# Attention keys in one ring tile, score pieces of up to 512 columns, and 64 weight columns for the lower part of some value blocks

## The chip, the cores and the metric

The kernel runs on one core of one Trainium2 chip. The metric is the device time of one execution in microseconds. A time is the median of several runs of the same kernel; the profile is one further execution, taken by the hardware profiler, with a time of its own.

## What is computed

One layer of a streaming encoder for 1024 prompt rows and 64 sample rows, all in float32, with 1024 channels. The change touches the two attentions of the prompt alone: eight heads of band attention (A) and eight heads of forgetting attention (B), each with 64 channels to a head.

```python
def attend(q, k, v, bias, mask):
    logits = jnp.einsum('bqhd,bkhd->bhqk', q, k).astype(jnp.float32) * scale
    ...
    p = jax.nn.softmax(logits, axis=-1)
    return jnp.einsum('bhqk,bkhd->bqhd', p.astype(v.dtype), v)
...
# A: each 64-frame chunk attends to itself and the 8 chunks before it, with a learned relative bias
# B: causal, swept in 128-query blocks, bias = cum[query] - cum[key] of the forget logits
oa = chunk_band_attn_prompt(qa, ka, va, rel_bias[l])
ob = forget_attn_prompt(qb, kb, vb, logf)
xp = xp + jnp.concatenate([oa, ob], axis=-1) @ w_o[l]
```

Before it stands the projection h @ w_in that makes q, k and v; behind it an output projection, a cross-attention into 256 memory tokens, and a feed-forward part with a short convolution.

## The kernel before

**Precision.** A float32 number is split into a higher part and a lower part ("hi" and "lo"), both of the type fp32r, which TensorE takes in one pass. A product of two split numbers is made of three matmuls (hi·hi, hi·lo, lo·hi); lo·lo is left out. In the attention the two halves of the array hold two such terms at once. A head has 64 channels, so the queries of one head stand as weights with hi in one half of the 128 partitions and lo in the other, against keys that have hi in both halves (z = 0) or lo in both (z = 1). For the values the two parts are two halves of the weight columns: v holds 64 columns of hi and 64 of lo, and the output has two halves of 64 partitions, which ACT and VectorE add at the end (L743, L744).

**Stages.** From about 30 to 545 us the eight head pairs (p = 0 to 3 are A, 4 to 7 are B) are projected, and the attention of one pair runs beside the projection of the next. From 545 us come the sample rows and the memory's keys and values, then the output projection, the cross-attention and the feed-forward part.

**One pair's attention.** The 1024 rows are eight blocks of 128. A `Group` is two blocks: its key tile `k` (L332) holds for both heads hi and lo of 256 keys, and five such tiles rotate. A group's keys are written by `group_turn` (L473 to L489): four transposes, ACT's copies (L482), VectorE's lower parts (L484), and two transfers by the SP queue (L485) that copy each head's keys to the other half of the partitions; then the queries (L487, L489). `Attn(p, g, h)` is one head's attention for the two query blocks of group g. `score(j)` (L659) makes the scores of one query block t against the key blocks w0 to t (for A at most five, for B all from the first): for each key group two matmuls (z = 0 and 1) with the same weights, of 256 columns, or of 128 where only one of the group's blocks is in the window (L677 to L682). They go into the PSUM tile `S` of two banks, of which there is one. VectorE adds the bias and takes the maximum (L685), ACT the exponential (L687), GpSimd scales (L689). `turn` (L719 to L721) transposes the weights of four key blocks at a time, and ACT and VectorE split them into pth and ptl. `sum` (L723) multiplies by the values: for each key block one matmul with pth and one with ptl, of 256 columns where both query blocks see the key block (the blocks of `self.full`), of 128 where one alone does.

**Order.** The code records the instructions; at the end `arrange` (L2050) plays them through with a table of costs and puts each engine's instructions up to the feed-forward part in the order in which that play issued them, with the program's order as priority. Its cost of a matmul (L2086) counts the columns that move, not the columns of the weights. SP issues all transfers in one queue.

Of the kernel before, what the change touches and what calls it, by code (L numbers as in the profile page):

```python
# [8 lines left out]
F32R = mybir.dt.float32r  # L9
# [6 lines left out]
P = 128  # L16
# [25 lines left out]
def hybrid_step(ctx: ExitStack, tc: tile.TileContext, i: dict, o: dict):  # L42
    nc = tc.nc
    act, dve, pool, pe = nc.scalar, nc.vector, nc.gpsimd, nc.tensor
# [56 lines left out]
    wa = heads.enter_context(tc.tile_pool(name="wa", bufs=1, side="right"))  # L101
# [225 lines left out]
    ramp.append(len(nc.cur_bb.bb.instructions))  # L327


    class Group:  # L330
        def __init__(self):
            self.k = wa.tile([P, 2, 2, 256], F32R, name="k", bufs=5)  # L332
            self.v = wa.tile([P, 2, 2, 2, 64], F32R, name="v", bufs=5)
            self.q = self.qk = None

    groups = {}
# [304 lines left out]

    mixes = {}

    class Attn:


# [12 lines left out]
        def score(self, j, sp=None):  # L659
            p, g, h = self.p, self.g, self.h  # L660
            w0, t = self.window(j)
            n = (t - w0 + 1) * P
            s = wk.tile([P, N], F32, name="s", bufs=4)
            self.s[j] = s
            if p >= 4:
                head = 2 * (p - 4) + h
                pool.tensor_scalar(s[:, :n], bias[p, h][:, :n], ctok[:, t, head:head + 1], 1.0, op0=ALU.add, op1=ALU.mult)
                pool.affine_select(out=s[:, n - P:n], in_=s[:, n - P:n], compare_op=ALU.is_ge, fill=NEG, base=0,
                                   pattern=[[-1, P]], channel_multiplier=1)
                b = s[:, :n]  # L670
            else:
                b = bias[p, h][:, 640 - n:640]
            if sp is None:
                sp = ps.tile([P, 2, 512], F32, name="S", bufs=1).rearrange("p a b -> p (a b)")
            off = (w0 % 2) * P
            q = groups[p, g].q[:, h, j * P:(j + 1) * P]
            for kg in range(w0 // 2, t // 2 + 1):  # L677
                k0, k1 = max(w0, 2 * kg), min(t, 2 * kg + 1) + 1
                a = off + (k0 - w0) * P
                src = slice((k0 - 2 * kg) * P, (k1 - 2 * kg) * P)  # L680
                for m in range(2):
                    pe.matmul(sp[:, a:a + (k1 - k0) * P], q, groups[p, kg].k[:, h, m, src], start=m == 0, stop=m == 1)  # L682
            mx = wk.tile([P, 1], F32, name="mx", bufs=4)
            sm = wk.tile([P, 1], F32, name="ssum", bufs=4)
            dve.tensor_tensor_reduce(out=s[:, :n], in0=sp[:, off:off + n], in1=b, scale=-1.0, scalar=BIG,  # L685
                                     op0=ALU.add, op1=ALU.min, accum_out=mx)
            act.activation(s[:, :n], s[:, :n], ACT.Exp, bias=mx, scale=-1.0, accum_out=sm)  # L687
            dve.reciprocal(sm, sm)  # L688
            pool.tensor_scalar(s[:, :n], s[:, :n], sm, 1.0, op0=ALU.mult, op1=ALU.mult)  # L689
# [33 lines left out]
        def sum(self, ch):  # L723
# [3 lines left out]
            if first:  # L727
                self.op = bank("O")[:, :256].rearrange("p (a b) -> p a b", a=2)
            op = self.op
            for b in sorted(ch, key=lambda b: (b != self.full[0], b)):  # L730
                cols = slice(0 if b <= a1 else 1, 2 if b >= b0 else 1)
                hi, lo, x = self.pts[b]
                for m, pt in enumerate((hi, lo)):
                    pe.matmul(op[:, cols], groups[p, b // 2].v[:, b % 2, h].rearrange("p a d -> p (a d)"),  # L734
                              pt[:, x, cols], start=b == self.full[0] and m == 0, stop=b == self.last and m == 1)
            if ch[-1] != self.last:
                return
            if h == 0:
# [767 lines left out]
    for n, u in enumerate(mems):  # L1506
        h, c = u.h, u.c
# [834 lines left out]
```

## Time and profile before

| | |
|---|---|
| median of 3 runs | 1707.46 us (1704.11 to 1709.73) |
| the profiled execution | 1703.21 us, span 1701.4 us |
| TensorE clock granted over the span | 0.998 |
| key transfers (L485) | 60, 128 KB each, 2.3 us from issue to landing |
| VectorE waiting for scores (L685 for L682) | 22.3 us in 44 waits |

The profile has for each engine a busy time, and for TensorE two rows: PE for matmuls and PEld for the loads of weights, which run beside the matmul ahead of them. Each matmul has its own weight load. Records of matmuls overlap, because they are pipelined: how long one holds the engine is read from the distance of starts, not from its duration. The views of the trace that are used below are windows (busy time of each engine in a stretch), groups by line, waits (who waited for whom), and the timeline. In a group's row "x160 | 28.2, 258 | 2.1" is the count, the busy time in us, the mean duration in ns, and the idle time ahead of it. In a timeline row the first two numbers are start and length in us, and a form `128*64` gives the rows and the columns of the weights.

### The profile page before, as it was taken

The page shows a single profiled execution, that of the slowest core. Times are in us where ns is not written, and L with a number is a line of the kernel's source. Part 1 is how long each engine was busy: PE and PEld are TensorE (multiplying, and loading weights), DVE is VectorE, ACT ScalarE, POOL GpSimd, SP SyncE. Part 2 cuts the span into 40 slices and gives each one's busy share as a digit, 9 for nine tenths or more (in the row PEclk, how much of TensorE's full clock was granted, in tenths as well). Part 3 has the DMA queues.
Part 4 walks back from the last instruction along what each step waited for, and adds up shares of the span by engine and source line. Part 5 has one row for each costly group of instructions (what it writes and reads, how often), then busy time and mean ns, then how long its engine had stood idle before and what let it go on. Part 6 is the DMA issues. An engine that isn't in the chain of part 4 may idle for free.

```text
span 1701.4 us, 33544 instructions
## 1 busy us (share of the span) xinstructions
PE 1676.9 (99%) x12264; PEld 1636.4 (96%) x12264; DVE 1158.1 (68%) x2552; ACT 906.8 (53%) x1995; POOL 583.3 (34%) x846
## 2 busy tenths in 40 slices
PE   8999999999999999999999999999999999999999
PEld 8899999999998889999999999999999999999998
DVE  7877766767777645334444697777777777659986
ACT  8757766767777565335555554333333333434442
POOL 1746647888877104434445211000000000000000
PEclk9999999999999999999999999999999999999999
DMA  8322223223146955411114642222222222983332
GB/s 258 101 57 81 75 81 103 76 77 99 48 147 189 267 186 185 139 57 51 55 58 141 211 134 83 80 78 79 77 77 77 77 79 82 306 305 122 104 108 88
DMA packets 138422, 199.84 MB, mean 117 GB/s; under 512 B 22200, under 2 KB 77624, under 8 KB 138256
## 3 DMA queue, kind: packets, MB, share of 16 engines
q1 hardware_dynamic: 138256, 197.70, 37.8%
q8 instruction: 96, 1.57, 0.4%
q14 instruction: 70, 0.57, 0.1%
HBM read 148.01 MB, written 43.34 MB: 112 GB/s over the span
## 4 chain that ended last, share of the span: by engine, by line
PE 83%; DVE 6%; ACT 5%; DMA 2%; issue 2%; POOL 1%; SPq 0%; DVEq 0%; ACTq 0%; POOLq 0%
PE W L1703 26%; PE pj L1156 14%; PE W L2027 11%; PE pj L407 11%; PE S L682 4%; PE O L734 3%; PE PT L719 3%; PE pj L802 2%; PE W L1156 2%; PE pj L529 1%; PE S L1445 1%; PE tq L1481 1%; PE O L1481 1%; PE O L1056 1%; ACT q L487 1%
## 5 line engine op out<-in xcount | busy, mean ns | idle before, releaser
L407 PE MATMUL pj<-whi,xhi 128*128 128x384 f32 (+1 forms) x480 | 175.4, 365 | 0.0
L407 PE MATMUL pj<-wlo,xhi 128*128 128x384 f32 (+1 forms) x480 | 164.7, 343 | 0.0
L407 PE MATMUL pj<-whi,xlo 128*128 128x384 f32 (+1 forms) x480 | 164.1, 342 | 0.0
L1703 PE MATMUL W<-h,hi 128*128 128x272 f32 x704 | 134.3, 288 | 1.4 <-ACT qlo L1839 1.4
L1809 POOL COPY s<-gp 128x2 f32<-128x2 f32 x22 | 15.8, 719 | 336.1 <-DVE gp L1808 336.1
L2027 PE MATMUL W<-f,hi 128*128 128x272 f32 x672 | 127.2, 287 | 0.1
L721 DVE TENSOR_TENSOR ptl<-PT,pth 128x512 fp32r<-128x512 f32 (+2 forms) x192 | 98.5, 521 | 37.1 <-ACT pth L720 34.4
L720 ACT CAST pth<-PT 128x512 fp32r<-128x512 f32 (+2 forms) x192 | 85.2, 450 | 57.9 <-PE PT L719 55.8
L689 POOL TENSOR_SCALAR s<-s,ssum 128x640 f32<-128x640 f32 (+7 forms) x128 | 92.0, 720 | 69.5 <-DVE ssum L688 59.2
L687 ACT ACTIVATE s<-s,mx 128x640 f32<-128x640 f32 (+7 forms) x128 | 94.4, 737 | 37.6 <-DVE mx L685 36.9
L1703 PEld LDWEIGHTS W<-h,hi 128*128 128x128 f32 x704 | 110.4, 188 | 1.7 <-ACT qlo L1839 1.6
L2027 PEld LDWEIGHTS W<-f,hi 128*128 128x128 f32 x672 | 105.3, 188 | 0.3 <-DVE f L1774 0.3
L1703 PE MATMUL W<-h,lo 128*128 128x272 f32 x352 | 101.4, 288 | 0.0
L682 PE MATMUL S<-k,q 128*128 128x256 f32 (+1 forms) x608 | 94.3, 283 | 6.9 <-DVE mx L685 4.5
L682 PEld LDWEIGHTS S<-k,q 128*128 128x128 f32 x608 | 83.9, 190 | 17.2 <-DVE mx L685 5.6
L2027 PE MATMUL W<-f,lo 128*128 128x272 f32 x336 | 96.7, 288 | 0.0
L1566 ACT CAST hi<-raw 128x512 fp32r<-128x512 f32 x68 | 42.3, 621 | 98.8 <-PE W L1703 59.2
L719 PE MATMUL PT<-ident,s 128*128 128x128 f32 x528 | 89.8, 275 | 3.2 <-DVE ptl L721 1.5
L407 PEld LDWEIGHTS pj<-whi,xhi 128*128 128x128 f32 x480 | 90.9, 189 | 1.2
L407 PEld LDWEIGHTS pj<-wlo,xhi 128*128 128x128 f32 x480 | 91.2, 190 | 0.1
L407 PEld LDWEIGHTS pj<-whi,xlo 128*128 128x128 f32 x480 | 90.4, 188 | 0.0
L1156 PE MATMUL pj<-a,hi 128*128 128x384 f32 (+1 forms) x352 | 87.3, 332 | 1.0 <-DVE a L1209 0.9
(608 smaller groups left out, 5716.1 us busy)
## 6 DMA issues: line engine op xcount, KB each, us to landing
raw<-in_w_down_dram SPq DMA_DIRECT2D x45, 256.0 KB, 2.8
wraw<-in_w_dram SPq DMA_DIRECT2D x56, 192.0 KB, 2.7
raw<-in_w_up_dram SPq DMA_DIRECT2D x41, 256.0 KB, 2.7
h<-ad SPq DMA_DIRECT2D x32, 272.0 KB, 5.2
mwraw<-in_w_mkv_dram SPq DMA_DIRECT2D x16, 512.0 KB, 5.0
raw<-in_w_mo_dram SPq DMA_DIRECT2D x32, 256.0 KB, 3.3
kvraw<-in_w_down_dram SPq DMA_DIRECT2D x32, 256.0 KB, 2.7
k<-k SPq DMA_DIRECT2D x60, 128.0 KB, 2.3
```

What stands on the lines that cost most here:

```text
L407: pe.matmul(pj[:, :nw], x_part(a, k, t * P, P), wt[k][b][:, :nw], start=n == 0, stop=n == 3 * KT - 1)
L682: pe.matmul(sp[:, a:a + (k1 - k0) * P], q, groups[p, kg].k[:, h, m, src], start=m == 0, stop=m == 1)
L687: act.activation(s[:, :n], s[:, :n], ACT.Exp, bias=mx, scale=-1.0, accum_out=sm)
L689: pool.tensor_scalar(s[:, :n], s[:, :n], sm, 1.0, op0=ALU.mult, op1=ALU.mult)
L719: pe.transpose(pt[:, b - ch[0]], self.s[j][:, (b - w0) * P:(b - w0 + 1) * P], ident)
L720: act.copy(hi[:, f:f + n, j], pt[:, f:f + n])
L721: dve.tensor_tensor(lo[:, f:f + n, j], pt[:, f:f + n], f32(hi[:, f:f + n, j]), op=ALU.subtract)
L734: pe.matmul(op[:, cols], groups[p, b // 2].v[:, b % 2, h].rearrange("p a d -> p (a d)"), pt[:, x, cols], start=b == self.full[0] and m == ...
L1156: pe.matmul(out()[:, :cn], w[a][:, k % 4], x[b][k][:, c0:c0 + cn], start=k == 0 and (a, b) == SPLIT[0], stop=k == KT - 1 and (a, b) == SPL ...
L1566: act.copy(hi, t)
L1703: pe.matmul(w[:, z, :Q], a(p, j), rights[j][b][:, z * Q:z * Q + Q], start=fresh and begin and j == 0 and x == 0, stop=final and end and j ...
L2027: pe.matmul(ws[m][:, z, :Q], la[p][:, m * P:(m + 1) * P], ra[b][:, z * Q:z * Q + Q], start=first and y == 0 and what in opening, stop=fina ...
```

## The change

It has three parts.

1. The five key tiles become one tile, `ring`, of five places of 256 keys. A group takes the next place in turn (`at`), and `self.k` is a slice of the ring. So the keys of groups that were made one after the other lie side by side, except over the ring's end.
2. `key_parts` cuts the key blocks of a window into pieces that lie side by side in the ring and do not cross a bank of `S`, up to 512 columns. It tries the places in `S` where the scores may begin and takes the cheapest by a count in which a piece of 128 columns costs as much as one of 256. (Pair 0's first groups share `S` between two heads; there the place is fixed.)
3. In `sum` the matmul with the lower part ptl, for key blocks that one query block alone sees, takes the 64 columns of v's higher part as its weights and writes 64 partitions; the product of the two lower parts, which it added before, is left out there. Those blocks come ahead of the blocks of `self.full`, behind the first matmul of the sum.

```diff
+    RING = 5
+    ring = wa.tile([P, 2, 2, RING * 256], F32R, name="k")
+    turns_of = []
...
-            self.k = wa.tile([P, 2, 2, 256], F32R, name="k", bufs=5)
+            self.at = len(turns_of) % RING
+            turns_of.append(self)
+            self.k = ring[:, :, :, self.at * 256:self.at * 256 + 256]
...
+    def key_parts(p, w0, t, bank_only):
+        where = [groups[p, b // 2].at * 256 + b % 2 * P for b in range(w0, t + 1)]
+        n = len(where)
+        best = None
+        for first in range(1 if bank_only else 9 - n):
+            cost, parts, x = 0, [], 0
+            while x < n:
+                m = 1
+                while x + m < n and where[x + m] == where[x] + m * P and (first + x + m) % 4:
+                    m += 1
+                parts.append(((first + x) * P, where[x], m * P))
+                cost += max(2, m)
+                x += m
+            if best is None or cost < best[0]:
+                best = cost, first * P, parts
+        return best[1:]
...
-            off = (w0 % 2) * P
...
-            for kg in range(w0 // 2, t // 2 + 1):
-                k0, k1 = max(w0, 2 * kg), min(t, 2 * kg + 1) + 1
-                a = off + (k0 - w0) * P
-                src = slice((k0 - 2 * kg) * P, (k1 - 2 * kg) * P)
-                for m in range(2):
-                    pe.matmul(sp[:, a:a + (k1 - k0) * P], q, groups[p, kg].k[:, h, m, src], start=m == 0, stop=m == 1)
+            off, parts = key_parts(p, w0, t, bank_only)
+            for a, k0, m in parts:
+                for z in range(2):
+                    pe.matmul(sp[:, a:a + m], q, ring[:, h, z, k0:k0 + m], start=z == 0, stop=z == 1)
...
-            for b in sorted(ch, key=lambda b: (b != self.full[0], b)):
+            steps = [(b, m) for b in sorted(ch, key=lambda b: (b in self.full, b)) for m in range(2)]
+            if first:
+                steps.sort(key=lambda x: x != (self.full[0], 0))
+            for b, m in steps:
...
-                for m, pt in enumerate((hi, lo)):
-                    pe.matmul(op[:, cols], groups[p, b // 2].v[:, b % 2, h].rearrange("p a d -> p (a d)"),
-                              pt[:, x, cols], start=b == self.full[0] and m == 0, stop=b == self.last and m == 1)
+                r = 64 if m and b not in self.full else P
+                pe.matmul(op[:r, cols], v[:, :r], self.pts[b][m][:, x, cols], start=first and (b, m) == steps[0], stop=ch[-1] == self.last and (b, m) == steps[-1])
```

Counted over the built programs, the score matmuls of the prompt are:

| columns of one | 128 | 256 | 384 | 512 | all | columns in all |
|---|---|---|---|---|---|---|
| before | 160 | 448 | 0 | 0 | 608 | 135168 |
| changed | 60 | 172 | 100 | 88 | 420 | 135168 |

Of the 608 value matmuls, 80 (ptl, 128 columns) go from 128 weight columns to 64. All other engines have as many instructions as before, and the copies of keys are still 60.

The next rows are TensorE's queue in pair 4, at a query block whose window holds all eight key blocks, first before; the value matmuls beside its scores belong to the unit ahead of it. L407 is the projection of the next pair, L682 the scores, L734 the values.

```order
L407 MATMUL pj<-wlo,xhi 128x384
L407 MATMUL pj<-whi,xlo 128x384
L734 MATMUL O<-pth,v 128x256
L682 MATMUL S<-k,q 128x256 x8
L734 MATMUL O<-ptl,v 128x256
L734 MATMUL O<-pth,v 128x128
L734 MATMUL O<-ptl,v 128x128
```

And the same place in the changed kernel, where L413, L704 and L760 are these three lines.

```order
L413 MATMUL pj<-wlo,xhi 128x384
L704 MATMUL S<-k,q 128x512 x4
L413 MATMUL pj<-whi,xlo 128x384
L760 MATMUL O<-pth,v 128x128
L760 MATMUL O<-ptl,v 64x128
L760 MATMUL O<-pth,v 128x256
L760 MATMUL O<-ptl,v 128x256
```

Eight score matmuls have become four, the 128-column pair of the values stands ahead of the 256-column pair, and its second matmul writes 64 partitions instead of 128.

The scores of seven key blocks are the other kind of place. Before, a few rows further on in TensorE's queue (L719 are transposes of attention weights):

```order
L682 MATMUL S<-k,q 128x256 x6
L682 MATMUL S<-k,q 128x128 x2
L407 MATMUL pj<-whi,xlo 128x384
L407 MATMUL pj<-whi,xhi 128x384
L407 MATMUL pj<-wlo,xhi 128x384
```

In the changed kernel (L741 are the transposes):

```order
L704 MATMUL S<-k,q 128x512 x2
L704 MATMUL S<-k,q 128x384 x2
L413 MATMUL pj<-whi,xhi 128x384
L413 MATMUL pj<-wlo,xhi 128x384
L413 MATMUL pj<-whi,xlo 128x384
L741 MATMUL PT<-ident,s 128x128 x4
```

The pair of 128 columns is gone, and the scores are two pieces of each part instead of four.

On SP's queue the key copies keep their places; each now copies two runs of 256 keys from a partition instead of one run of 512. Before:

```order
L554 DMA sv<-vf 64x128
L485 DMA k<-k 64x512 x2
L128 DMA wraw<-in_w_dram 128x384 x2
L553 DMA sqk<-qk 64x256
L551 DMA out_bk_dram<-ko 64x128
```

In the changed kernel (L491 is the copy of keys):

```order
L560 DMA sv<-vf 64x128
L491 DMA k<-k 64x2x256 x2
L128 DMA wraw<-in_w_dram 128x384 x2
L559 DMA sqk<-qk 64x256
L557 DMA out_bk_dram<-ko 64x128
```

More of the change, by code (lines that the diff above doesn't have):

```diff
@@ L672, in score @@
                 b = bias[p, h][:, 640 - n:640]
+            bank_only = sp is not None
             if sp is None:
                 sp = ps.tile([P, 2, 512], F32, name="S", bufs=1).rearrange("p a b -> p (a b)")
-            off = (w0 % 2) * P
             q = groups[p, g].q[:, h, j * P:(j + 1) * P]
-            for kg in range(w0 // 2, t // 2 + 1):
-                k0, k1 = max(w0, 2 * kg), min(t, 2 * kg + 1) + 1
-                a = off + (k0 - w0) * P
-                src = slice((k0 - 2 * kg) * P, (k1 - 2 * kg) * P)
-                for m in range(2):
-                    pe.matmul(sp[:, a:a + (k1 - k0) * P], q, groups[p, kg].k[:, h, m, src], start=m == 0, stop=m == 1)
+            off, parts = key_parts(p, w0, t, bank_only)
+            for a, k0, m in parts:
+                for z in range(2):
+                    pe.matmul(sp[:, a:a + m], q, ring[:, h, z, k0:k0 + m], start=z == 0, stop=z == 1)
             mx = wk.tile([P, 1], F32, name="mx", bufs=4)
@@ L729, in sum @@
             op = self.op
-            for b in sorted(ch, key=lambda b: (b != self.full[0], b)):
+            steps = [(b, m) for b in sorted(ch, key=lambda b: (b in self.full, b)) for m in range(2)]
+            if first:
+                steps.sort(key=lambda x: x != (self.full[0], 0))
+            for b, m in steps:
                 cols = slice(0 if b <= a1 else 1, 2 if b >= b0 else 1)
-                hi, lo, x = self.pts[b]
-                for m, pt in enumerate((hi, lo)):
-                    pe.matmul(op[:, cols], groups[p, b // 2].v[:, b % 2, h].rearrange("p a d -> p (a d)"),
-                              pt[:, x, cols], start=b == self.full[0] and m == 0, stop=b == self.last and m == 1)
+                v = groups[p, b // 2].v[:, b % 2, h].rearrange("p a d -> p (a d)")
+                x = self.pts[b][2]
+                r = 64 if m and b not in self.full else P
+                pe.matmul(op[:r, cols], v[:, :r], self.pts[b][m][:, x, cols], start=first and (b, m) == steps[0], stop=ch[-1] == self.last and (b, m) == steps[-1])
             if ch[-1] != self.last:
```

## The prediction, made before the changed kernel ran

> **What bounds the kernel now.** I read the page first: busy times, slices, and the chain that ended last.
>
> ```profile
> span 1701.4 us, 33544 instructions
> PE 1676.9 (99%) x12264; PEld 1636.4 (96%) x12264; DVE 1158.1 (68%) x2552; ACT 906.8 (53%) x1995; POOL 583.3 (34%) x846
> ...
> PE 83%; DVE 6%; ACT 5%; DMA 2%; issue 2%; POOL 1%; SPq 0%; DVEq 0%; ACTq 0%; POOLq 0%
> PE W L1703 26%; PE pj L1156 14%; PE W L2027 11%; PE pj L407 11%; PE S L682 4%; PE O L734 3%; PE PT L719 3%; PE pj L802 2%; PE W L1156 2%; PE pj L529 1%; PE S L1445 1%; PE tq L1481 1%; PE O L1481 1%; PE O L1056 1%; ACT q L487 1%
> ```
>
> TensorE is the bound, and the lines that the change touches, L682 and L734, are on the chain. A busy PE is modelled, so I asked next for windows of the stage.
>
> ```profile
> core 0: us, PE busy (x) PEld busy (x) DVE busy (x) ACT busy (x) POOL busy (x), PEclk, DMA share, GB/s
> 30.00:545.00 515.00, 503.20 (x3440) 479.83 (x3439) 370.65 (x1035) 365.69 (x945) 373.09 (x580) 1.00 0.34 94
> 130.00:480.00 350.00, 348.75 (x2403) 335.19 (x2402) 245.35 (x677) 247.07 (x631) 264.87 (x417) 1.00 0.31 86
> 410.00:480.00 70.00, 69.92 (x487) 67.30 (x486) 49.26 (x130) 47.91 (x118) 60.23 (x100) 1.00 0.33 96
> 1100.00:1400.00 300.00, 300.00 (x2396) 300.00 (x2396) 225.96 (x387) 116.56 (x171) 26.36 (x58) 1.00 0.24 77
> ```
>
> In the attention stage, 30 to 545 us, PE stands idle for 11.8 us, and between 130 and 480 us for 1.25 us. So what TensorE no longer does there comes off the time, if nobody else becomes late. POOL is the next busiest: 60.23 of 70 us in pairs 4 to 7.
>
> **What one matmul holds of TensorE** is the distance of starts. The timeline at 300 us has the value matmuls, and at 302 us three projections in a row.
>
> ```profile
> 300.14 0.28 PE L734 MATMUL O<-pth,v 128*128 128x256 f32 x1
> 300.26 0.28 PE L734 MATMUL O<-ptl,v 128*128 128x256 f32 x1
> 300.37 0.23 PE L734 MATMUL O<-pth,v 128*128 128x128 f32 x1
> ...
> 300.26 0.19 PEld L734 LDWEIGHTS O<-pth,v 128*128 128x128 f32 x1
> 300.38 0.19 PEld L734 LDWEIGHTS O<-ptl,v 128*128 128x128 f32 x1
> 300.49 0.19 PEld L407 LDWEIGHTS pj<-whi,xhi 128*128 128x128 f32 x1
> 300.60 0.19 PEld L407 LDWEIGHTS pj<-wlo,xhi 128*128 128x128 f32 x1
> ...
> 302.46 0.34 PE L407 MATMUL pj<-wlo,xhi 128*128 128x384 f32 x1
> 302.64 0.34 PE L407 MATMUL pj<-whi,xlo 128*128 128x384 f32 x1
> 302.81 0.38 PE L719 MATMUL PT<-ident,s 128*128 128x128 f32 x2
> ```
>
> Loads of 128 weight columns follow each other at 0.11 us even where the matmul between them moves 128 columns (300.38, 300.49, 300.60). So a matmul of 128 columns costs 0.11 us: the load binds. 256 columns cost 0.118 (0.59 us for the five steps from 775.78 to 776.37, rows below). 384 cost 0.175 (302.46 to 302.81, two steps). The columns bind there, at 0.057 us for 128 more. This fits 272 columns: 300 us over 2396 matmuls, 0.125. No fp32r matmul of 512 columns is in the trace; by the same slope it is 0.232, which I take. Bounds: not under 0.175, the price of 384, and not over two of 256, 0.236.
>
> The Trainium skill (TensorE: Matmul & The Clock Gate, Back-to-back issue gap) has N/2.4 + 2.5 ns, which is 0.216 us for 512 columns. With it the 88 long pieces would save 1.4 us more; but for 384 it says 0.163 where the trace has 0.175, so the trace's slope stands.
>
> **The change, part by part.** The counts of the matmuls that change:
>
> ```profile
> L682 PE MATMUL S<-k,q 128*128 128x256 f32 x448 | 76.4, 293 | 4.8 <-DVE mx L685 3.6 <-DVE q L489 0.2
> L682 PE MATMUL S<-k,q 128*128 128x128 f32 x160 | 28.2, 258 | 2.1 <-DVE mx L685 0.9 <-DMA k<-k 0.9 <-DVE q L374 0.3
> L734 PE MATMUL O<-ptl,v 128*128 128x128 f32 x80 | 22.1, 276 | 0.0
> ```
>
> *Scores.* Before: 160 x 0.11 + 448 x 0.118 = 70.5 us. After: 60 x 0.11 + 172 x 0.118 + 100 x 0.175 + 88 x 0.232 = 64.8 us. That is **-5.7 us**, nearly all of it from the hundred 128-column pieces that join longer ones: alone they cost 0.11, in a longer piece 0.057. Joining two of 256 saves 0.004. With the bounds of 512 it is -10.7 to -5.3.
>
> *Values.* 80 matmuls load 64 columns instead of 128. Such a load in a stretch of 128-column matmuls is not in the trace for fp32r; these rows are nearest, the scores of the cross-attention for 64 rows:
>
> ```profile
> 775.61 0.34 PE L1156 MATMUL pj<-hhi,lo 128*128 128x384 f32 x1
> 775.78 0.28 PE L1445 MATMUL O<-kSh,qhi 128*64 128x256 f32 x1
> ...
> 776.37 0.28 PE L1445 MATMUL O<-kSh,qlo 128*64 128x256 f32 x1
> 776.49 0.36 PE L1156 MATMUL pj<-hhi,hi 128*128 128x384 f32 x1
> 776.68 0.35 PE L1156 MATMUL pj<-hlo,hi 128*128 128x384 f32 x1
> 776.87 0.34 PE L1156 MATMUL pj<-hhi,lo 128*128 128x384 f32 x1
> ...
> 775.79 0.14 PEld L1445 LDWEIGHTS O<-kSl,qhi 128*64 128x64 f32 x1
> ```
>
> The load's record is 0.14 instead of 0.19 us: 0.05 less. Going to 64 columns is free (775.61 to 775.78 is the 384 columns of the matmul ahead). Coming back costs nothing at once, and then 0.19 and 0.19 instead of 0.175 twice, 0.03 in all. If the load takes 0.055, the pth matmul ahead of it holds TensorE for its own 0.057 instead of 0.11, while the ptl matmul keeps 0.11, since the next load has 128 columns again. That is 0.05 each, 80 x 0.05 = **-4.0 us**; with the slow return -1.6. The other end is rival three. That these blocks come first changes no count; they wait for the same pth and ptl.
>
> *The ring.* A piece that holds the newest keys now waits for their copy where before only the last pair of matmuls did; that pair began up to 0.7 us later. The copy takes 2.3 us, and as two runs of 1 KB instead of one of 2 KB it has its nearest row in mixd (128 rows of 1 KB, 2.0 us): no difference.
>
> ```profile
> k<-k SPq DMA_DIRECT2D x60, 128.0 KB, 2.3
> ...
> mixd<-mix SPq DMA_DIRECT2D x32, 128.0 KB, 2.0
> ...
> PEld S L682 <- DMA k<-k: 1.1, 1, 1.1
> ```
>
> Today two waits for keys are seen, 0.9 (the L682 row above) and 1.1 us. Only where the first piece holds the newest group does it bite, about one group of the four in each pair; 16 heads x one such group x 0.7 us = 11 us is the most, but `arrange` knows the copy and puts projections ahead, so I take **+0.5**. The queue behind such a wait is TensorE's next projection, and nobody but its eviction waits for that.
>
> *Everything else.* The other engines do the same work in 9 us less. POOL goes from 86% to about 88% in pairs 4 to 7; some of TensorE's saved time becomes waiting: **+0.5**, 5% of it.
>
> The sum is -5.7 - 4.0 + 0.5 + 0.5 = **-8.7 us**. Against the profiled execution (span 1701.4, 1703.2 in all) that is 1694.5. The median of the runs shown is 4.3 us above that execution, so I forecast 1707.5 - 8.7 = **1698.8 us**.
>
> **Rivals.** *One: a load of 64 columns costs as much as one of 128.* A transpose has it:
>
> ```profile
> 577.67 0.42 PEld L1056 LDWEIGHTS O<-vraw,pth 128*128 128x128 f32 x3
> 578.00 0.11 PEld L1042 LDWEIGHTS PT<-ident,s 128*64 128x64 f32 x1
> 578.12 0.19 PEld L802 LDWEIGHTS pj<-mwhi,mhi 128*128 128x128 f32 x1
> ```
>
> From the 64-column load at 578.00 to the next at 578.12 pass 0.12 us, as between loads of 128. Against it: this is a transpose of plain float32. Then the values give nothing, -5.7 + 1.0 = -4.7, or 1702.8.
>
> *Two: the cover is gone in pairs 4 to 7.* If GpSimd's chain (86% busy) paces those pairs once TensorE is faster, their half of the 9.7 us returns as waits: about -4, 1703.5. Against it: PE had 0.08 us of idle time in 410 to 480, so projections fill every hole.
>
> *Three, the other side: changing between 128 and 64 weight columns empties the array.* The sums of squares of the cross-attention (plain float32, two matmuls to each product) show that:
>
> ```profile
> 774.52 0.41 PEld L1426 LDWEIGHTS PT<-ones,sq 128*128 128x128 f32 x3
> 774.94 0.19 PEld L1426 LDWEIGHTS PT<-ones,sq 128*64 128x64 f32 x2
> 775.15 0.19 PEld L1156 LDWEIGHTS pj<-hhi,hi 128*128 128x128 f32 x1
> ```
>
> Three loads of 128 are 0.11 apart, the last at 774.74; the next would start at 774.85 but starts at 774.94, 0.09 late. Two of 64 are 0.055 apart, so the return is due at 775.05 and comes at 775.15, 0.10 late. The 80 matmuls each go there and back: 80 x 0.19 = 15.2 us more, and the sum is -8.7 + 15.2 = +6.5, or 1714. It decides from 8.7 / 80 = 0.11 us a round trip on. Against it: L1445, fp32r as here, goes in free and returns for 0.03, and a wait for an empty array can't hide behind the matmul that it waits for.
>
> The Trainium skill says it as a rule (TensorEngine Tiling (Array Packing), Key Properties): a change of the tiling mode drains TensorE, and it lists 128x64 as a mode. L1426 agrees with it, L1445 does not.
>
> **How the numbers follow.** Forecast 0.55, rival one 0.22, two 0.10, three 0.13. About 0.3%, 5.1 us, is what a measurement of this kernel can tell from no change. The forecast is faster by more than that but for the slow return with more waits (0.06 of its 0.55); rivals one and two lie at that bound, about 0.4 of their 0.32 beyond it: faster 0.62, same 0.25, slower 0.13. The range holds the forecast, both milder rivals and the medians' own scatter of 3 us: 1692 to 1709; rival three is left out.
>
> **What would show it.** In the changed profile L704 has 420 matmuls, and 512 columns start 0.23 us apart; behind a 64-column load of L760 the next load starts after 0.06 us and not 0.11 (rival one), and the 64-column load itself starts with the matmul ahead of it, not 0.09 late (three). PE's idle time between 130 and 480 us stays near 1 us; rival two would make it 5. The output projection begins some 9 us sooner. The forecast is wrong if waits of L704 for keys or for the one `S` tile add up to several us.

## The result and the profile after

The changed kernel took **1697.27 us** (median of 6 runs, 1694.44 to 1699.68), the kernel before in the same rounds 1705.78 us (6 runs, 1702.28 to 1710.38). The ratio is **0.9947, 95% interval 0.9932 to 0.9962**: 8.5 us less by the medians. In a later set it was 0.9935 (0.9920 to 0.9950). The forecast was 8.7 us less. The total was right; the experiments show that several of its terms were not, so that the total agrees in part by luck.

The page of the changed kernel, first the busy times, then the chain that ended last:

```profile
span 1695.6 us, 33195 instructions
PE 1671.0 (99%) x12076; PEld 1622.1 (96%) x12076; DVE 1157.5 (68%) x2552; ACT 906.3 (53%) x1995; POOL 583.5 (34%) x846
...
PE 83%; DVE 7%; ACT 5%; DMA 3%; issue 2%; POOL 1%; SPq 0%; DVEq 0%; ACTq 0%; POOLq 0%
PE W L1728 26%; PE pj L1181 14%; PE W L2052 14%; PE pj L413 10%; PE S L704 3%; PE O L760 3%; PE PT L741 2%; PE pj L827 2%; PE S L1470 1%; DVE s L707 1%; PE tq L1506 1%; PE O L1506 1%; PE pj L535 1%; PE O L1081 1%; DVE ptl L743 1%
```

The profiled execution's span is 5.8 us shorter. The score matmuls fell from 4% to 3% of the chain, and two lines of VectorE that were not among those named before have come into it: L707, which takes the scores out of `S`, and L743, which makes ptl. The windows of the same stretches of the changed kernel say the same in another way:

```profile
core 0: us, PE busy (x) PEld busy (x) DVE busy (x) ACT busy (x) POOL busy (x), PEclk, DMA share, GB/s
...
130.00:480.00 350.00, 346.67 (x2285) 326.77 (x2284) 241.54 (x678) 245.36 (x631) 266.77 (x420) 1.00 0.32 88
410.00:480.00 70.00, 69.77 (x479) 66.91 (x479) 48.34 (x130) 47.31 (x117) 60.98 (x100) 1.00 0.36 104
```

Between 130 and 480 us TensorE was idle for 1.25 us before and is idle for 3.33 us now, although PE's row is modelled and hides short waits. GpSimd went from 60.23 to 60.98 of 70 us. TensorE's matmuls by shape, from the groups of the changed kernel (count, busy time, mean ns, then idle time ahead):

```profile
L704 PE MATMUL S<-k,q 128*128 128x256 f32 x172 | 33.7, 293 | 0.8 <-DVE mx L707 0.4
L704 PE MATMUL S<-k,q 128*128 128x384 f32 x100 | 28.6, 364 | 2.0 <-DMA k<-k 1.6 <-DVE q L495 0.2
L704 PE MATMUL S<-k,q 128*128 128x512 f32 x88 | 28.1, 412 | 1.3 <-DVE mx L707 1.0
L760 PE MATMUL O<-ptl,v 128*64 128x128 f32 x80 | 19.0, 237 | 0.7 <-DVE ptl L743 0.7
...
L704 PE MATMUL S<-k,q 128*128 128x128 f32 x60 | 11.2, 266 | 2.0 <-DVE mx L707 1.4 <-DVE q L380 0.3
```

The counts are those of the prediction. Of the idle time ahead of the scores, 1.6 us for key copies stand ahead of pieces of 384 columns, and 1.0 us for VectorE ahead of those of 512. Over the whole kernel it did not grow: it adds up to 6.1 us in these rows, against 6.9 us in the rows of L682 before. The timeline of matmuls shows what 512 columns cost:

```profile
302.62 0.62 PE L704 MATMUL S<-k,q 128*128 128x512 f32 x2
303.08 0.34 PE L413 MATMUL pj<-whi,xhi 128*128 128x384 f32 x1
```

Two of them take 0.46 us, 0.23 each.

**How TensorE's time is accounted for below.** A load starts when the matmul ahead of it starts, so the distance between the starts of two loads is what one matmul holds. Each matmul up to the output projection was given this distance as *held* time, as long as it is at most 0.012 us over the median of its shape and of the next load's width; where it is more, the mean of its kind counts as held and the rest as *wait*. Work and waits up to the output projection then add up to the time at which that begins. The table has, for every run, the ratio to the kernel before with its interval, the start of the first output projection matmul in the profiled execution, held time of scores and values, and the waits in two stretches, between 150 and 450 us and from 500 us to the output projection (all in us).

| run | ratio to before | output projection | scores held | values held | waits 150 to 450 | waits from 500 |
|---|---|---|---|---|---|---|
| before | 1 | 631.65 | 70.2 | 70.2 | 10.7 | 15.1 |
| changed | 0.9947 (0.9932 to 0.9962) | 625.01 | 64.2 | 67.3 | 16.9 | 13.3 |
| scores alone | 0.9951 (0.9935 to 0.9968) | 623.90 | 64.6 | 70.0 | 14.5 | 11.0 |
| sums alone | 0.9965 (0.9954 to 0.9976) | 624.93 | 69.8 | 67.1 | 12.0 | 10.3 |
| ring alone | 1.0005 (0.9994 to 1.0016) | 631.63 | 70.2 | 70.3 | 11.4 | 13.4 |
| all lower parts 64 | 0.9965 (0.9953 to 0.9977) | 625.30 | 64.5 | 67.2 | 16.4 | 15.5 |
| changed, 128 columns | 0.9955 (0.9943 to 0.9967) | 625.08 | 64.2 | 70.3 | 14.5 | 12.6 |
| order of sums alone | 0.9966 (0.9955 to 0.9978) | 625.97 | 69.9 | 70.2 | 10.9 | 10.5 |
| planner's price | 0.9964 (0.9950 to 0.9978) | 626.73 | 64.1 | 67.1 | 16.7 | 13.9 |
| fewer projections | 0.9868 (0.9854 to 0.9882) | 607.26 | 64.0 | 67.5 | 17.2 | 10.3 |
| short projections | 0.9915 (0.9900 to 0.9930) | 618.98 | 64.3 | 67.3 | 29.3 | 11.9 |
| short values | 0.9924 (0.9910 to 0.9937) | 620.89 | 64.1 | 49.6 | 23.7 | 13.9 |
| changed, second time | 0.9935 (0.9920 to 0.9950) | 623.40 | 64.4 | 67.2 | 16.4 | 11.4 |
| 128 columns, second time | 0.9949 (0.9935 to 0.9963) | 623.27 | 64.2 | 70.2 | 13.9 | 11.7 |

At the output projection the two profiles of the changed kernel differ by 1.6 us, and the two with 128 columns by 1.8, so a single profile is good to some 2 us there. Ring alone has the instructions and the order of the kernel before on TensorE, and its waits from 500 us are 13.3 us against 15.1: a figure of that column moves by some 2 us between two executions.

### The profile page after: what moved, and what is told of

Same layout as the page of the kernel before. It is cut to its first block, busy times and chain, and to the rows that moved or that the text cites. A ratio compares the mean times of both kernels' runs of the same rounds, so it can differ in the third digit from the quotient of the medians.

```text
span 1695.6 us, 33195 instructions
## 1 busy us (share of the span) xinstructions
PE 1671.0 (99%) x12076; PEld 1622.1 (96%) x12076; DVE 1157.5 (68%) x2552; ACT 906.3 (53%) x1995; POOL 583.5 (34%) x846
## 4 chain that ended last, share of the span: by engine, by line
PE 83%; DVE 7%; ACT 5%; DMA 3%; issue 2%; POOL 1%; SPq 0%; DVEq 0%; ACTq 0%; POOLq 0%
PE W L1728 26%; PE pj L1181 14%; PE W L2052 14%; PE pj L413 10%; PE S L704 3%; PE O L760 3%; PE PT L741 2%; PE pj L827 2%; PE S L1470 1%; DVE s L707 1%; PE tq L1506 1%; PE O L1506 1%; PE pj L535 1%; PE O L1081 1%; DVE ptl L743 1%
## 5 line engine op out<-in xcount | busy, mean ns | idle before, releaser
L413 PE MATMUL pj<-whi,xhi 128*128 128x384 f32 (+1 forms) x480 | 173.2, 361 | 0.0
L413 PE MATMUL pj<-whi,xlo 128*128 128x384 f32 (+1 forms) x480 | 165.4, 345 | 0.0
L413 PE MATMUL pj<-wlo,xhi 128*128 128x384 f32 (+1 forms) x480 | 164.3, 342 | 0.0
L743 DVE TENSOR_TENSOR ptl<-PT,pth 128x512 fp32r<-128x512 f32 (+2 forms) x192 | 98.4, 522 | 34.8 <-ACT pth L742 32.1
L704 PE MATMUL S<-k,q 128*128 128x256 f32 (+3 forms) x420 | 92.2, 331 | 6.0 <-DVE mx L707 2.8
L413 PEld LDWEIGHTS pj<-whi,xhi 128*128 128x128 f32 x480 | 91.0, 190 | 1.5
L741 PE MATMUL PT<-ident,s 128*128 128x128 f32 x528 | 89.3, 275 | 2.8 <-DVE ptl L743 1.2
L413 PEld LDWEIGHTS pj<-wlo,xhi 128*128 128x128 f32 x480 | 91.2, 190 | 0.5
L413 PEld LDWEIGHTS pj<-whi,xlo 128*128 128x128 f32 x480 | 90.7, 189 | 0.4
L704 PEld LDWEIGHTS S<-k,q 128*128 128x128 f32 x420 | 67.2, 190 | 21.7 <-DVE q L495 7.3
```

The lines of the kernel that those rows point to most:

```text
L413: pe.matmul(pj[:, :nw], x_part(a, k, t * P, P), wt[k][b][:, :nw], start=n == 0, stop=n == 3 * KT - 1)
L704: pe.matmul(sp[:, a:a + m], q, ring[:, h, z, k0:k0 + m], start=z == 0, stop=z == 1)
L741: pe.transpose(pt[:, b - ch[0]], self.s[j][:, (b - w0) * P:(b - w0 + 1) * P], ident)
L743: dve.tensor_tensor(lo[:, f:f + n, j], pt[:, f:f + n], f32(hi[:, f:f + n, j]), op=ALU.subtract)
```

## The experiments

### One part at a time: scores alone, sums alone, ring alone

Scores alone keeps the ring and `key_parts` and has the old `sum`; sums alone has the old key tiles and score pieces and the new `sum`; ring alone has neither.

```diff
 scores alone, in sum:
-            steps = [(b, m) for b in sorted(ch, key=lambda b: (b in self.full, b)) for m in range(2)]
...
+            for b in sorted(ch, key=lambda b: (b != self.full[0], b)):
 ring alone, in score as well:
-            off, parts = key_parts(p, w0, t, bank_only)
-            for a, k0, m in parts:
...
+            off = (w0 % 2) * P
...
+            for kg in range(w0 // 2, t // 2 + 1):
```

> The ring and the long score pieces of the change, with the value sums as before (128 weight columns, old order). Theory (scores -5.7, values -4.0, waits and cover +1.0): -5.7 + 0.5 + 0.3 = about -5 us against before, ratio near 0.997; the profile has 88 matmuls of 512 columns about 0.23 us apart and PE idle of 130 to 480 us up by 1 to 2 us. Rival one (the values gave nothing): all of the change's 8.5 us is here, ratio 0.995. Rival B (long pieces are eaten by waits for keys, so that the values or the order gave the gain): 0 to -2 us.

> The keys and score pieces as before, the new value sums alone (80 ptl matmuls of 64 weight columns, lo times lo left out there, these blocks ahead of the blocks that both query blocks see). Theory: 80 x 0.05 = -4.0 us less some 0.3 of waits, about -3.7, ratio near 0.998; the load behind a 64-column load starts 0.06 us after it. Rival one (a 64-column load costs as much as one of 128): 0, ratio 1.000. Rival three (the change of weight columns empties the array): +11 to +15 us, which the changed kernel's time already speaks against.

> The keys in one ring tile and nothing else: score pieces and value sums as before. Theory: the copies of keys land as fast as before (two runs of 1 KB instead of one of 2 KB), no wait comes or goes: 0, within 0.5 us. Rival: the ring itself costs (copies with twice as many packets, a coarser wait for the whole tile): +1 to +3 us, with waits of the scores for keys above 3 us; or it gains by chance of the order, -1 to -2.

Scores alone took 1696.12 us against 1703.95, sums alone 1698.73, ring alone 1705.76. No cost of the ring shows: the interval of its ratio is 0.9994 to 1.0016, its output projection begins at the same time as before, and its copies of keys, with two runs of 1 KB, land in 2.4 us where those with one run of 2 KB took 2.3 (profile of ring alone):

```profile
k<-k SPq DMA_DIRECT2D x60, 128.0 KB, 2.4
```

The other two don't add up. By the ratios scores alone gives 8.3 us and sums alone 6.0, together 14.3, but the kernel with both gains 9.0 (and 11.1 the second time; the intervals of the three ratios leave that smaller shortfall open). Neither expectation was met as it stood: scores alone is at the number of rival one, sums alone beyond the theory's. The table shows what they have in common. Scores alone has 5.6 us less held time, sums alone 3.1 in the values, as the theory had it; but both also have less waiting from 500 us on, 4 to 5 us less than before and 2 to 3 less than ring alone, which no term spoke of.

### More short loads

In this kernel every matmul with `ptl` takes 64 weight columns, 304 instead of 80, and the lower part comes first within a block, so that a sum doesn't end with 64 columns.

```diff
-            steps = [(b, m) for b in sorted(ch, key=lambda b: (b in self.full, b)) for m in range(2)]
+            steps = [(b, m) for b in sorted(ch, key=lambda b: (b in self.full, b)) for m in (1, 0)]
...
+                if steps[-1][1]:
+                    steps.insert(1, steps.pop())
...
-                r = 64 if m and b not in self.full else P
+                r = 64 if m else P
```

> The changed kernel, with 64 weight columns for all 304 ptl matmuls instead of 80: 224 more, all of 256 moving columns, where the product of the two lower parts is now left out as well; within each block the lower part comes first. Theory (a matmul holds TensorE for the longer of the next load and its own columns, and 256 columns are 0.118 against a load of 0.11): nothing gained, and a return from 64 to 128 columns costs up to 0.03, so 0 to +6.7 us against the changed kernel, 1697 to 1704. Rival (each 64-column load saves 0.05 wherever it stands): -11, about 1686. Rival three (the change of columns empties the array, and something else hid it in the changed kernel): 224 x 0.19 = +43, 1740.

It took 1698.08 us, ratio 0.9965 (0.9953 to 0.9977), some 3 us more than the changed kernel by the ratios (each is good to about 2 us), within the theory's span. The 304 short loads save no more held time than the 80 did: 67.2 us against 67.3. Only 54 of them stand behind a value matmul of 128 columns; 180 stand behind one of 256, which holds TensorE for about 0.118 us before either load (the medians are 0.117 to 0.119). The empty array of rival three is out: it would have been 43 us.

### 64 against 128 weight columns in the same order

The planner's cost of a matmul does not count weight columns, so with 128 columns everywhere all engines keep their order, and nothing but the width of 80 loads differs (and with it the product of the two lower parts, which is added again there).

```diff
-                r = 64 if m and b not in self.full else P
+                r = P
```

> The changed kernel with 128 weight columns in all value matmuls: the same instructions in the same order on TensorE, 80 of them with wider weights; the product of the two lower parts is added again there. Theory (a matmul holds TensorE for the longer of its own columns and the next load, so a 64-column load pays only where the matmul ahead of it moves 128 columns, which in the changed kernel's trace is so for 55 of 80): 55 x 0.05 = +2.7 us against the changed kernel, about 0.9963 of before, and the 0.06 us slots become 0.11. By the prediction's own term: +4.0. Rival (the 64-column loads save nothing): 0, ratio 0.995.

The same place in the loads of the two kernels, first the changed one, then the one with 128 columns:

```profile
457.52 0.19 PEld L760 LDWEIGHTS O<-pth,v 128*128 128x128 f32 x1
457.69 0.13 PEld L760 LDWEIGHTS O<-ptl,v 128*64 128x64 f32 x1
457.75 0.19 PEld L760 LDWEIGHTS O<-pth,v 128*128 128x128 f32 x1
457.86 0.19 PEld L760 LDWEIGHTS O<-ptl,v 128*128 128x128 f32 x1
```

```profile
457.81 0.19 PEld L760 LDWEIGHTS O<-pth,v 128*128 128x128 f32 x1
457.98 0.19 PEld L760 LDWEIGHTS O<-ptl,v 128*128 128x128 f32 x1
458.09 0.19 PEld L760 LDWEIGHTS O<-pth,v 128*128 128x128 f32 x1
458.20 0.19 PEld L760 LDWEIGHTS O<-ptl,v 128*128 128x128 f32 x1
```

Behind the 64-column load the next load starts after 0.06 us (457.69 to 457.75), behind the 128-column one after 0.11. Coming back to 128 columns costs nothing: 457.75 to 457.86 is 0.11 in both. The Trainium skill (TensorE: Matmul & The Clock Gate, LDWEIGHTS) gives a load P/1.2 ns for P columns, by which 128 and 64 columns are estimated at 0.107 and 0.053 us; the trace, with 0.11 and 0.06, agrees. The Trainium skill's rule that a change of the tiling mode drains TensorE (TensorEngine Tiling (Array Packing), Key Properties) does not show in these loads.

But this happened for 55 of the 80 only. In the other 25 the order puts something else between `pth` and `ptl`: 11 times a transpose, which holds TensorE for 0.109 us ahead of either load, and otherwise a projection or a score matmul of 256 to 512 columns, nearly all of which hold it for as long as ahead of a load of 128. So the values hold 67.3 us instead of 70.3, 3.0 less.

And in the profiles almost nothing of these 3.0 us reached the end of the stage. The output projection begins at 625.01 with 64 columns and at 625.08 with 128; in the second pair at 623.40 and 623.27. Since the order is the same, the n-th load of one profile can also be set against the n-th of the other. 52 of the 55 places lie between 62 and 500 us, 2.6 us by their price; over that stretch the changed kernel gets ahead of the one with 128 columns by 0.3 to 0.5 us in either pair. The waits are longer instead: between 150 and 450 us 16.9 against 14.5, and 16.4 against 13.9. One place shows how a lead can be lost. These are matmuls, the SP queue and VectorE at a group's scores in the changed kernel (a queue row of SP is the time that issuing takes):

```profile
204.20 0.50 PE L704 MATMUL S<-k,q 128*128 128x256 f32 x2
205.84 0.62 PE L704 MATMUL S<-k,q 128*128 128x384 f32 x2 [1.14 <-DMA k<-k]
...
201.27 1.65 SPq L128 DMA_DIRECT2D wraw<-in_w_dram  x1
203.01 1.36 SPq L491 DMA_DIRECT2D k<-k  x2
...
201.69 0.49 DVE L490 SCALAR_TENSOR_TENSOR k<-tq,gd,k 64x256 fp32r<-64x256 f32 x1
```

And with 128 columns:

```profile
204.57 0.50 PE L704 MATMUL S<-k,q 128*128 128x256 f32 x2
205.76 0.61 PE L704 MATMUL S<-k,q 128*128 128x384 f32 x2 [0.69 <-DMA k<-k]
...
201.60 1.26 SPq L128 DMA_DIRECT2D wraw<-in_w_dram  x1
202.96 1.36 SPq L491 DMA_DIRECT2D k<-k  x2
...
202.02 0.49 DVE L490 SCALAR_TENSOR_TENSOR k<-tq,gd,k 64x256 fp32r<-64x256 f32 x1
```

With the short loads TensorE gets to the scores 0.37 us sooner (204.20 against 204.57), and VectorE has the keys ready 0.33 sooner. The copies of keys start at the same time all the same, 203.01 and 202.96, because the SP queue is still issuing a transfer of weights ahead of them. So TensorE waits 1.14 us instead of 0.69, and goes on at 205.84, no sooner than the other at 205.76. Why that issue took 1.65 us here is not shown, and it is not the short loads' doing by this evidence: in the second pair it took 1.51 us with 64 columns and 0.53 with 128, so there the wait is the changed kernel's alone (0.83 us), and the kernel with 128 columns ran through its scores from 203.77 on without a listed wait of its matmuls. The place shows that a queue can take a lead back; that this is what happens to the short loads in general is argued from the longer waits.

The times leave the question open: the ratios are 0.9947 against 0.9955, and 0.9935 against 0.9949 in the second pair. That pair ran in the same rounds, and its medians are 2.6 us apart (1693.35 and 1695.98); the twelve times put the difference of the means between 0.8 and 3.9 us (95% interval).

> The changed kernel itself, as the reference for the runs at its order. Its ratio to before should be 0.9947 as measured, within 0.0015.

> Again the changed kernel with 128 weight columns in all value matmuls, now in the same rounds as the changed kernel. Theory Q: 2.7 us slower than it (ratio to it 1.0016). Theories P and R: at most 1 us slower, or no difference.

The second pair's times look like theory Q, its profiles like P: the two differ by 1.4 us of span (1692.1 and 1693.5), all of it behind the output projection, where the two programs are the same; two executions of the changed kernel differ there by 1.9 us as well. So what the 64 columns bring stays open between next to nothing (the profiles) and about their price (the second pair's times).

### The order of the sums alone

This is the kernel before with the new order of the steps in `sum`, and 128 columns everywhere; it has the same order on TensorE as sums alone.

```diff
-            for b in sorted(ch, key=lambda b: (b != self.full[0], b)):
+            steps = [(b, m) for b in sorted(ch, key=lambda b: (b in self.full, b)) for m in range(2)]
+            if first:
+                steps.sort(key=lambda x: x != (self.full[0], 0))
+            for b, m in steps:
...
+                r = P
```

> The kernel before with the new order of the value steps alone, all with 128 weight columns: the order of instructions of the run with the new sums alone, which took 5.9 us less than before. Theory: its 55-odd short loads gave 2.7 us, and the rest (3 us) came from waits that the new order of all engines happens to avoid, so -3 us here, ratio 0.998. Rival (the order is worth nothing, the loads are worth all): 0, ratio 1.000. Rival (the loads are worth nothing): -5.9, ratio 0.9965.

It took 1697.63 us, ratio 0.9966 (0.9955 to 0.9978): 5.8 us less, and as much as sums alone (0.9965). It does exactly the matmuls of the kernel before. So nearly all of the gain of sums alone is order; the third line of the expectation holds. The width adds 0.2 us by the two ratios, good to 2.7, and 1.0 us at the output projection (624.93 against 625.97), within the scatter. The granted clock was a little higher in these five runs than in the kernel before (0.9996 against 0.9978 on the mean). Within the runs of one kernel 0.001 of it goes with some 1.2 us, so up to 2 us of the 5.8 may be the clock's. The start of the output projection, 5.7 us sooner, shows no such dependence: ring alone, granted 1.0 in its profile, reached it at 631.63 us, the kernel before, granted 0.998, at 631.65.

Held time is the same (70.2 us). Of the 5.7 us, 4.6 are waits from 500 us on (15.1 to 10.5; 2.8 against ring alone's 13.3), the stretch in which the last pair's attention runs out beside the sample rows. Between 150 and 450 us nothing changes (10.7 and 10.9). Three waits account for much of it, here in the kernel before:

```profile
536.13 0.44 PE L682 MATMUL S<-k,q 128*128 128x128 f32 x2 [0.86 <-DMA k<-k]
555.22 0.66 PE L719 MATMUL PT<-ident,s 128*128 128x128 f32 x4 [0.79 <-DVE ptl L721]
568.17 0.58 PE L950 MATMUL PT<-ident,kv 128*128 128x128 f32 x2 [1.67 <-DVE mms L929]
```

Ring alone, in the old order, has the same three. With the new order of the sums the first two are not there, and the third, ahead of the transposes of the memory's keys, is 0.6 to 0.8 us (sums alone and order of sums alone).

### The planner's price of a short matmul

```diff
-                o = max(0.087, 0.003 + cols * 0.000456)
+                o = max(0.111, 0.003 + cols * 0.000456)
```

> The changed kernel with one number of the planner changed: the least cost of a matmul, 0.111 instead of 0.087 (the trace has 0.11 for 128 columns). The computation is the same, the order differs in places. Theory (the order of the whole stage moves the waits by a few us either way, whatever it was changed for): within 3 us of the changed kernel, sign open. Rival (the planner's price is what cost the changed kernel its added waits of 3 to 4 us): -3 to -4 us against it, ratio 0.993 of before.

It took 1698.40 us, ratio 0.9964 (0.9950 to 0.9978), not faster than the changed kernel. The rival falls: a truer price of 128 columns doesn't recover the waits (16.7 us between 150 and 450). The output projection begins 1.7 us later than in the changed kernel's first profile at the same held time: another order of the same work.

### Less work for TensorE, planned anew and in a fixed order

If waits follow from the order, then a saving that the planner sees and one that it doesn't should differ. The first kernel leaves out 80 projection matmuls, and everything is planned again.

```diff
-            pe.matmul(pj[:, :nw], x_part(a, k, t * P, P), wt[k][b][:, :nw], start=n == 0, stop=n == 3 * KT - 1)
+            pe.matmul(pj[:, :nw], x_part(a, k, t * P, P), wt[k][b][:, :nw], start=n == 0, stop=n == keep[-1])
...
+        keep = [n for n in range(3 * KT) if not (2 <= p <= 6 and n >= 18 and n % 3 == 1)]
+        return pj, pieces(len(keep), 3, lambda j: one(keep[j]))
```

> The changed kernel with 2 of 24 matmuls left out of each projection of pairs 2 to 6 (higher part of the rows times lower part of the weights, in the last two eighths of the channels): 80 matmuls of 384 columns, 80 x 0.175 = 14.0 us of TensorE in the stage where the attention runs. Theory A (TensorE has no cover left to lose, waits are chance of the order): all of it comes off, -14 us within 3, 1683 us by the changed kernel's median. Theory B (the attention's own chain paces part of the stage, and over half of what TensorE saves there returns as waits, as +6 us of waits between 150 and 450 us for 10 us saved suggest): -4 to -7 us, 1690 to 1693, with PE's idle time between 130 and 480 us up from 3.3 to 10 us or more.

It took 1681.46 us, ratio 0.9868 (0.9854 to 0.9882). Against the changed kernel's two ratios that is 11 to 13 us of 14.0; the output projection begins 16 to 18 us sooner in a profile that fell on the fastest of the four runs. Theory A holds: TensorE is the bound, and no other engine paces the stage. The windows say so too: TensorE is idle for 3.5 us, as in the changed kernel, though all others are busier (GpSimd 273.38 instead of 266.77 us). How much of the gain is the new order's own, which was worth 5.8 us in the run above, isn't separated.

```profile
130.00:480.00 350.00, 346.51 (x2290) 325.62 (x2289) 251.53 (x707) 255.28 (x659) 273.38 (x436) 1.00 0.33 92
```

The other two keep every engine in the changed kernel's order, which was written into them as a list. One shortens 240 projection matmuls, the other nearly all value matmuls of the blocks that both query blocks see.

```diff
 short projections:
-            pe.matmul(pj[:, :nw], x_part(a, k, t * P, P), wt[k][b][:, :nw], start=n == 0, stop=n == 3 * KT - 1)
+            w = 128 if 2 <= p <= 6 and k >= 2 and n % 3 == 1 else nw; pe.matmul(pj[:, :w], x_part(a, k, t * P, P), wt[k][b][:, :w], start=n == 0, stop=n == 3 * KT - 1)
 short values:
+                r, cols = (64, slice(0, 1)) if b in self.full and (b, m) != (self.full[0], 0) and (ch[-1] != self.last or (b, m) != steps[-1]) else (64 if m and b not in self.full else P, cols)
 both, in arrange:
+    order = _given_order(order)
```

> The changed kernel with all engines in exactly its order, and 240 projection matmuls of pairs 2 to 6 (higher part of the rows times lower part of the weights, six of the eight eighths of the channels) of 128 columns instead of 384, so that this product is left out for two thirds of the columns. By the price of a matmul (the longer of its columns and the next load, 0.175 to 0.11) TensorE holds 15.9 us less. Theory P (a queue in fixed order gives the time back at its next wait: with 64 against 128 weight columns at the same order 3.0 us of held time were 0.1 to 1.0 us of stage): at most 8 of the 15.9 us come off. Theory Q (those two comparisons were within the scatter, and TensorE's time counts in full): -14 to -16 us against the changed kernel.

> The changed kernel with all engines in exactly its order, and the value matmuls of the blocks that both query blocks see (all but the first and the last of each sum) with 64 weight columns and 128 moving columns instead of 128 and 256: a part of the output is left out. By the same price TensorE holds 17.1 us less. Theory P: at most 8 us come off, as with the projections. Theory Q: -15 to -17 us. Theory R (time saved in the value matmuls alone is lost, since they stand beside the waits of the scores, while projection time counts): 8 us at most here and 14 to 16 in the run with short projections.

In the same rounds the changed kernel took 1693.35 us. Short projections took 1690.30, short values 1691.84: **3.1 of 15.9 us and 1.5 of 17.1 us came off.** (The ratios, 0.9915 and 0.9924 against 0.9935, say 3.4 and 1.9.) The profiles say more: set load against load between 62 and 500 us, short projections gain 5.6 to 6.0 us on the two profiles of the changed kernel, and short values 4.2 to 4.7. By either measure it is well under half, so theory P holds, and R falls, since projections don't come near 14 us. The windows from 130 to 480 us of these two, short projections first:

```profile
130.00:480.00 350.00, 341.22 (x2327) 320.12 (x2327) 246.62 (x690) 249.82 (x642) 268.95 (x425) 1.00 0.32 89
```

```profile
130.00:480.00 350.00, 343.12 (x2319) 318.73 (x2319) 246.07 (x686) 249.43 (x639) 269.25 (x423) 1.00 0.31 88
```

TensorE is idle for 8.8 and 6.9 us here. What it waits for is in the groups of the score matmuls in that stretch, of the kernel before, the changed one, and the one with short projections:

```profile
L682 PE MATMUL S<-k,q 128*128 128x256 f32 (+1 forms) x426 | 64.2, 280 | 1.1 <-DVE mx L685 0.3
```

```profile
L704 PE MATMUL S<-k,q 128*128 128x256 f32 (+3 forms) x290 | 62.0, 327 | 3.0 <-DMA k<-k 1.6 <-DVE mx L707 0.5 <-DVE q L495 0.2
```

```profile
L704 PE MATMUL S<-k,q 128*128 128x256 f32 (+3 forms) x292 | 63.4, 330 | 7.8 <-DMA k<-k 3.6 <-DVE q L495 3.0 <-DVE mx L707 0.9
```

The same three waits grow in every case: for the copies of keys, for the queries, for `S` to be read. The first two are chains that start with TensorE's own transposes and go through ACT and VectorE (and for the keys through SP's queue) back to TensorE; the third goes from TensorE's scores through VectorE, which takes them out of the one `S` tile, to the next scores. The planner put projections and values between the two ends of a chain by its prices. Where these get shorter in a fixed order, TensorE is at the far end sooner and waits.

Not run: short projections with the order planned anew. That planning, and not another difference between leaving out and shortening, is what lets the first kernel keep its 14 us is therefore argued, not shown.

## Why the prediction was right

**What bounds the kernel.** "What TensorE no longer does there comes off the time, if nobody else becomes late." The bound is right: fewer projections, planned anew, bring 11 to 13 of 14.0 us. The condition is where it failed: in the middle of the stage TensorE's own chains are late at once.

**Scores, -5.7 us.** Right as a price. Held time of the score matmuls went from 70.2 to 64.2 us, 6.0 less, and 512 columns cost the 0.23 us that the slope had given. How much of it reached the time can't be taken alone, because fewer matmuls are also another order: scores on top of the new sums bring 3 to 5 us (0.9965 to 0.9947 and 0.9935), or 2 to 3 with 128 columns (0.9966 to 0.9955 and 0.9949); each of these differences is good to some 3 us.

**Values, -4.0 us: the mis-sized term.** The price of 0.05 us a load was right, the slow return was not there, and rivals one and three (a short load costs as much; the array empties) are out by 0.06 us from the short load to the next. The count was wrong. "The pth matmul ahead of it" is ahead of it in the code, but in TensorE's queue for 55 of 80 only; that gave 3.0 us of held time. The rows of the order stood in the part on the change, and a count over them would have shown it. And in a fixed order the profiles have these 3.0 us back as waits (about 4 us more of them up to the output projection, in both pairs of profiles); the times of the second pair, 2.6 us apart, don't bear that out, so how much of this term reached the time stays open.

**"That these blocks come first changes no count; they wait for the same pth and ptl." The term that was missed.** It was put at nothing, and it is the larger part of what the sums bring: order alone gives 5.8 us. Half of it or more comes from waits that the old order has from 500 us on (15.1 and 13.3 us in its two profiles, 10.3 and 10.5 with the new sums), the three shown above among them. The changed kernel has 13.3 and 11.4 there. That an order can avoid these waits only once would explain why scores alone and sums alone don't add up; this is argued, not shown, as is what in the old order made them.

**The ring and waits for keys, +0.5.** The ring alone costs 0 (0.9994 to 1.0016). The waits of longer pieces for keys are there as foreseen, 1.6 us in the stretch of the middle pairs against too little to be listed before. The two waits for keys of today, 0.9 and 1.1 us, are one: the row at 536.13 us above is the matmul's view of it, and the load's view of the same wait is 1.07 us. The sign that was to speak against the forecast, waits of L704 for keys or for `S` of several us, reads 4.4 us in the rows of the result; but it was 5.4 before, so it could not tell the two apart.

**Cover and waits of others, +0.5: too small.** Waits between 150 and 450 us rose by 5.7 to 6.2 us, for about 9 us less held time of scores and values. The prediction took 5% of the savings for them. Rival two, "the cover is gone", was the nearest to what happened; but not as it was put. It isn't GpSimd that paces, nor pairs 4 to 7 alone: most of the growth lies between 130 and 370 us, and next to none between 410 and 480, where TensorE is idle for 0.23 us. The 5 us of idle time that were to show that rival became 3.3, against some 1 us by the forecast.

**The sum.** At the output projection the changed kernel's first profile is 6.6 us ahead, the second 8.3; "some 9 us sooner" was nearly so. By the table: scores -6.0 and -5.8, values -2.9 and -3.0, waits between 150 and 450 us +6.2 and +5.7, waits from 500 us on -1.8 and -3.7 (0 and -1.9 against ring alone's profile); the other 1.5 to 2 us lie outside these columns. So in the profiles the total agrees by luck in part: fewer waits from 500 us on, which were not foreseen and which the new order of the sums brings also by itself, stand in for savings that went into longer waits in the middle of the stage.

## What to carry to other kernels

On an engine that is busy all the time, the price of an instruction says what it holds, not what comes off: in a queue whose order is fixed, a shorter filler brings TensorE sooner to the next wait on its own chain (here 1.5 to 3 of 16 to 17 us came off by the times, and 4 to 6 up to 500 us by the profiles). Let the order be planned again with the saving in it (that this is what kept the 11 to 13 of 14 us is argued, not shown), and test a saving by changing the work at the same order and the order at the same work, since an order alone can be worth as much as the change. Where a gain depends on what stands ahead of an instruction, count the neighbours in the queue as built, not in the source.

## What the runs showed of the hardware

- A 64-column load of fp32r weights between loads of 128 columns takes 0.06 us, and no extra time shows on the way in or back. Behind the plain float32 matmuls of L1426 in the kernel before, which the prediction's rival three went by, the loads came 0.09 and 0.10 us late at the same change of width; why they did is not shown.
- In these traces an fp32r matmul holds TensorE for the longer of its own columns and the next load: 0.06 us or less, 0.118, 0.175 and 0.231 us for 128, 256, 384 and 512 columns, against 0.11 for a load of 128 and 0.06 for one of 64. So 224 more short loads gave nothing: 54 of the 304 stand behind a value matmul of 128 columns, as 55 of the 80 did. A transpose of 128 columns held 0.109 us ahead of a 64-column load too.
- The part from the output projection on, the same matmuls in the same order in all these programs, took between 1068.7 us (changed, second time) and 1071.0 us (order of the sums alone) in profiles. Two executions of one program, the changed kernel, took 1068.7 and 1070.6 us: they differ there by nearly as much as the 64 columns could bring.
